# Expert stage of a two-layer diffusion block: another order of experts, one fixed in place of two, and 22 standing load places in place of 16

## Chip, cores and metric

One core of a Trainium2 chip. The metric is device time in microseconds (us) of one execution; less is better. Besides it there is one profiled execution of the kernel before, whose span runs from its first to its last instruction.

## What is computed

Two layers on 256 latent tokens of width 1024 (and 256 context tokens in the first). A layer is a mixer (linear attention beside neighbourhood attention) and a channel mixer. The change lies in the channel mixer of the second layer, a top-2-of-8 SwiGLU expert layer on the 256 latent tokens:

```python
def moe_swiglu(h, w_router, wg, wu, wd):
    def per_sample(t):
        logits = (t @ w_router).astype(jnp.float32)
        top_v, top_i = lax.top_k(logits, TOP_K)            # TOP_K = 2
        wts = jax.nn.softmax(top_v, axis=-1)
        combine = jnp.einsum('tk,tke->te', wts, jax.nn.one_hot(top_i, N_EXPERTS, ...))
        hid = jax.nn.silu(jnp.einsum('td,edf->tef', t, wg)) * jnp.einsum('td,edf->tef', t, wu)
        return jnp.einsum('tef,efd->td', hid * combine[:, :, None], wd)
```

Each of the 8 experts has three float32 matrices: gate and up 1024 x 3584, down 3584 x 1024. All 8 are read once, in units of 128 x 1024 numbers (524,288 bytes): 28 units a matrix, 84 an expert, 672 in all, 352.3 MB. After the layer follow a post-norm, a gate and the residual.

## The kernel before

**The stage.** `moe` (L1635) ends the second layer's mixer (its output projection, `out_w.run`), routes the tokens (`Router`), and then runs one `Stream` (L176) over the 672 units in the order that `Experts.jobs` (L1436) lists. A unit is loaded by SP (`wraw`, L161) into a place, and places are handed out in turn from a ring, `st.ring`; a place is free again when its unit has been read. SP issues the loads in the order of its own list, so one load that waits for its place holds back those behind it.

**Two ways to compute an expert.** *Split*: a unit is cut by ScalarE into a rounded part `wr` (L169) and by VectorE into the rest `wl` (L170), three units ahead of TensorE (`AHEAD = 3`), and six 128x512 matmuls (`mm3`, L210 to L212) multiply the two parts with the expert's tokens, which stand split in regions of `HR` and `HL` (up to 128 tokens an expert). A place is free once the unit is split. *Whole*: for an expert with at most 64 tokens, TensorE multiplies the unit as it is with 64 columns (`sides`, L1481); the trace shows four matmul records a unit. Neither ScalarE nor VectorE reads the unit, and its place is free only when TensorE has read it.

**The order.** The first `FIXED = 2` positions are experts 0 and 1. The other six are sorted by their number of tokens (`Router.rank`, L1277, which the stage steps through beside the units); `RANKS` says which rank comes at which position: few, many, few, many, few, many. "Few" positions run whole. So the order is split, split, whole, split, whole, split, whole, split. An expert from position 2 on is known to SP only by a register (`values_load` in `with_side`, L1443), read after unit 16 of the second position.

**Side work of an expert.** `gather` (L1423) picks two experts' tokens by one-hot matmuls (8 steps of four matmuls 128x256) during an earlier expert: experts 2 and 3 during the second position, 4 and 5 and then 6 and 7 during the whole ones at positions 2 and 4. The first two experts' tokens are picked together before the stage's first unit (`first`, L1389, with 256 columns). `scatter` (L1598) brings an expert's result back to its tokens; its 8 matmuls run after the second unit of the next expert, and for the last expert at once.

**Places.** 11 places are there from the mixer. At the start come 4 in pool `rm3`, 3 in `rm4`, the two accumulators, and one in `gtb`: 21. After unit 72 of the first expert `make_room` (L1724) takes the 3 in `rm4` and the 2 accumulators out: 16 from there on.

Of the kernel before, what the change touches and what calls it, by code (L numbers as in the profile page):

```python
# [25 lines left out]
FIXED = 2  # L26
RANKS = 3, 0, 4, 1, 5, 2
HALF = 64

# [58 lines left out]
ROOM_UNIT, GATHER_UNIT = 72, 32  # L88
IDS_UNIT, WHOLE_GATHER = 16, 12
RING = 4  # L90
# [3 lines left out]
def kernel(ctx: ExitStack, tc: tile.TileContext, A: dict, out: bass.AP):  # L94
# [188 lines left out]
    HR = pers.tile([P, KD, NT], F32R, name="HR")  # L283
    HL = pers.tile([P, KD, NT], F32R, name="HL")
# [847 lines left out]
    class Router:  # L1132
# [144 lines left out]
        def rank(self, pool):  # L1277
# [6 lines left out]
            def scratch():  # L1284
                return pool.tile([P, 256], F32, tag="hg", bufs=2, name="hg")

            at = scratch()[:, 0:n * n].rearrange("p (a b) -> p a b", a=n)
# [9 lines left out]
            t = scratch()[:, 0:7 * n * n].rearrange("p (q a b) -> p q a b", q=7, a=n)  # L1297
            nc.vector.tensor_tensor(out=t, in0=self.Q[:, :, FIXED:NE].unsqueeze(2).to_broadcast([P, 7, n, n]),
                                    in1=at.unsqueeze(1).to_broadcast([P, 7, n, n]), op=ALU.mult)
            nc.vector.tensor_reduce(out=self.T[:, :, FIXED:NE], in_=t, axis=AX.X, op=ALU.add)  # L1300
            yield
# [3 lines left out]
            nc.vector.tensor_scalar(out=b, in0=rank, scalar1=2.5, scalar2=-float(P - HALF), op0=ALU.is_gt, op1=ALU.mult)  # L1305
# [15 lines left out]
    class Experts:  # L1321
# [9 lines left out]
        def small(self, e):  # L1331
            return not self.rest and e >= FIXED and e % 2 == 0
# [8 lines left out]
        def region(self, e):  # L1341
            at = ((e // 2 + 1) % 2) * 256 + (e % 2) * P
            return slice(at, at + P)

        def one_hot(self, p, tts=(0, 1)):
            R, mg = self.R, self.R.mg
            for tt in tts:
                G = mg.tile([P, 2, P], F32R, tag=f"G{tt}", bufs=2, name=f"G{tt}")
                for i in range(2):
                    e = 2 * p + i  # L1350
# [4 lines left out]
                    eng, pin = (nc.gpsimd if tt else nc.vector, keep_order) if p else (nc.vector, lambda ins: ins)  # L1355
                    pin(eng.tensor_scalar(out=o, in0=io, scalar1=pos, scalar2=sel, op0=ALU.is_equal, op1=ALU.mult))
                self.G[tt] = G

        def pick(self, pg, d, tt, part, start, stop):
            nc.tensor.matmul(pg, self.R.x[tt][part][:, d * P:(d + 1) * P], self.G[tt].rearrange("p e s -> p (e s)"),  # L1360
                             start=start, stop=stop, skip_group_check=True)

        def picked(self, pg, p, d):
            at, n = self.region(2 * p).start, 256
            sc, sh = self.sc[:, d, 0:1], self.sh[:, d, 0:1]
            if self.small(2 * p):
                if d == 0:
                    self.xw[2 * p] = self.ml.tile([P, KD, HALF], F32, tag="xw", bufs=2, name="xw")
                nc.scalar.activation(self.xw[2 * p][:, d, :], pg[:, 0:HALF], AF.Identity, scale=sc, bias=sh)
                at, n, pg = at + P, P, pg[:, P:256]  # L1370
            o = (slice(None), d, slice(at, at + n))
            nc.scalar.activation(HR[o], pg, AF.Identity, scale=sc, bias=sh)
            h = self.ml.tile([P, 256], F32, tag="hg", bufs=2, name="hg")[:, 0:n]
            nc.vector.tensor_scalar(out=h, in0=pg, scalar1=sc, scalar2=sh, op0=ALU.mult, op1=ALU.add)
            nc.vector.tensor_tensor(out=HL[o], in0=h, in1=HR[o].bitcast(F32), op=ALU.subtract)

        def places(self, p):
            pt = ps()
            for i in range(2):
                for tt in range(2):  # L1380
                    o = (2 * i + tt) * P
                    nc.tensor.transpose(pt[:, o:o + P], self.G[tt][:, i, :].bitcast(F32), ident)
            gt = self.ml.tile([P, 2, 256], F32R, tag="GT", bufs=2, name="GT")
            nc.scalar.activation(gt.rearrange("p a t -> p (a t)"), pt, AF.Copy)
            self.GT[2 * p], self.GT[2 * p + 1] = gt[:, 0, :], gt[:, 1, :]
# [12 lines left out]
        def first_picked(self, places):  # L1398

            at = self.region(0).start  # L1400
            hs = [t.rearrange("p (d t) -> p d t", d=4)[:, 2 * j:2 * j + 2, :] for t in places for j in range(2)]
# [10 lines left out]
            def split(q):  # L1412
                o = (slice(None), slice(2 * q, 2 * q + 2), slice(at, at + 256))
                nc.scalar.activation(HR[o], hs[q], AF.Copy)
                nc.vector.tensor_tensor(out=HL[o], in0=hs[q], in1=HR[o].bitcast(F32), op=ALU.subtract)
# [7 lines left out]
        def gather(self, p):  # L1423
            self.one_hot(p)
            yield
            for d in range(KD):
                pg = ps()[:, 0:256]
# [3 lines left out]
                self.picked(pg, p, d)  # L1431
                yield
            self.places(p)
            yield
# [9 lines left out]
        def with_side(self, fn, e, i):  # L1444

            def g(wr, wl):
# [4 lines left out]
                if not self.rest and e == 0 and i == ROOM_UNIT:  # L1451
                    self.make_room()
                    self.places(0)
                    self.ranking = chain(self.R.weights(), self.R.rank(self.ml))
                next(self.ranking, None)
                if not self.rest and e == 1 and i == IDS_UNIT:
                    self.ids = [nc.values_load(self.R.ids[0:1, p:p + 1], engines=[mybir.EngineType.SP], min_val=0, max_val=NE - 1)
                                for p in range(NE - FIXED)]
# [3 lines left out]
                p, at = e // 2 + 1, WHOLE_GATHER if self.small(e) else GATHER_UNIT  # L1462
                if 2 * p < NE and (self.small(e) or e % 2 == 1 and (self.rest or e < FIXED)):
                    if i == at:
                        self.filler = self.gather(p)
                    if i >= at and i % 4 == 0:
                        next(self.filler, None)
# [9 lines left out]
        def expert(self, e):  # L1477
            slot, small = self.region(e), self.small(e)
            st = {}

# [30 lines left out]
            def gu(fbs, which, u, n):  # L1511
                def fn(wr, wl):
# [3 lines left out]
                    for b, fb in enumerate(fbs):  # L1516
                        for k2 in range(2 // len(fbs)):
                            kk = u * 2 // len(fbs) + k2
                            s = slice((b + k2) * 512, (b + k2 + 1) * 512)
                            if not small:  # L1520
                                mm3(st[fb, which], HR[:, kk, slot], HL[:, kk, slot], wr[:, s], wl[:, s], kk == 0, kk == KD - 1)
# [8 lines left out]
            def turn_whole(fbs):  # L1530
# [6 lines left out]
                for c in range(2 * n):  # L1537
                    st[fbs[0] * 4 + c, "x"] = t[:, c % n * P + c // n * HALF:c % n * P + (c // n + 1) * HALF]

# [58 lines left out]
        def scatter(self, e, ys):  # L1598
            small = self.small(e)
            yr = self.ml.tile([P, D], F32R, tag="yr", name="yr")  # L1600
            yl = self.ml.tile([P, D], F32R, tag="yl", name="yl")
            for half, y in enumerate(ys):
                c = slice(half * 512, (half + 1) * 512)
                nc.scalar.activation(yr[:, c], y, AF.Copy)
# [418 lines left out]
```

## Time and profile before

| | us |
|---|---|
| median of 3 runs (1928.47 to 1930.82) | 1930.63 |
| the profiled execution | 1930.77 |
| its span, first to last instruction | 1928.9 |
| expert stage: first unit's first matmul | 1003.2 |
| last expert's last unit ends on TensorE | 1914.2 |

The page gives busy time by engine and the span in 40 slices of 48.2 us. A busy TensorE there is not one at its peak, since ends of matmuls are modelled. In the expert stage the row to read beside it is GB/s, and for a stretch of one's choice the windows view (busy time by engine, granted TensorE clock, share of the DMA engines, GB/s).

### The profile page before, as it was taken

To read this page: it belongs to the slowest core of one execution; us is meant where nothing else is said; L and a number is where in the kernel's file an instruction comes from. 1 tells how busy PE (TensorE), PEld (TensorE's weight loads), DVE (VectorE), ACT (ScalarE), POOL (GpSimd) and SP (SyncE) were. 2 spreads that over 40 slices of the span, in tenths; PEclk is the share of its full clock that TensorE was granted. 3 is DMA by queue.
4 is the path that set the end of the run, shared out by engine and by line. 5 is a ranking of instruction groups with operands and counts; after the bars stand their busy time and mean duration, and the time that the engine had idled before them with its cause. 6 is when DMAs were issued, how large, how long until landed. Compare 5 with 4: busy or idle time off the path is not lost. (4 is left out here: it accounts for less than half of the span.)

```text
span 1928.9 us, 25373 instructions
## 1 busy us (share of the span) xinstructions
PE 1836.1 (95%) x8929; PEld 1296.1 (67%) x8929; DVE 1129.3 (59%) x1617; ACT 927.2 (48%) x1326; POOL 110.9 (6%) x111
## 2 busy tenths in 40 slices
PE   6999899999999998998989999998999989998997
PEld 3677557867888887786478878832786348832685
DVE  4456886432223335468789989820995149910897
ACT  4433366422222336443568778710774137710775
POOL 2001300100000002002100010100000000000000
PEclk9999999999999999999999999999999999999999
DMA  8521646175332332323889889999999999999993
GB/s 288 160 82 42 200 147 224 64 231 177 96 98 89 120 112 89 115 78 114 283 308 382 314 309 365 346 386 404 409 404 386 407 405 409 404 387 404 409 403 144
DMA packets 202182, 491.55 MB, mean 255 GB/s; under 512 B 28992, under 2 KB 70720, under 8 KB 202048
## 3 DMA queue, kind: packets, MB, share of 16 engines
q1 hardware_dynamic: 200768, 485.67, 69.2%
q0 software_dynamic: 1280, 4.20, 0.8%
q8 instruction: 72, 1.18, 0.2%
q14 instruction: 62, 0.51, 0.1%
HBM read 488.75 MB, written 4.19 MB: 256 GB/s over the span
## 5 line engine op out<-in xcount | busy, mean ns | idle before, releaser
L170 DVE TENSOR_TENSOR wl<-raw,wr 128x1024 fp32r<-128x1024 f32 x514 | 623.1, 1242 | 268.1 <-ACT wr L169 259.1
L169 ACT ACTIVATE wr<-raw 128x1024 fp32r<-128x1024 f32 x514 | 536.1, 1059 | 340.4 <-PE ps L211 135.3
L211 PE MATMUL ps<-wl,HR 128*128 128x512 f32 x736 | 291.4, 396 | 13.3 <-DVE wl L170 13.2
L210 PE MATMUL ps<-wr,HR 128*128 128x512 f32 x736 | 298.6, 406 | 3.9 <-ACT wr L169 3.9
L212 PE MATMUL ps<-wr,HL 128*128 128x512 f32 x736 | 291.8, 397 | 0.0
L210 PE MATMUL ps<-HR,wr 128*128 128x512 f32 (+1 forms) x592 | 222.2, 376 | 12.8 <-ACT HR L1863 6.0
L211 PE MATMUL ps<-HL,wr 128*128 128x512 f32 (+1 forms) x592 | 219.8, 371 | 3.4 <-POOL HL L424 1.8
L212 PE MATMUL ps<-HR,wl 128*128 128x512 f32 (+1 forms) x592 | 218.5, 369 | 0.0
L211 PEld LDWEIGHTS ps<-wl,HR 128*128 128x128 f32 x736 | 139.7, 190 | 50.2 <-DVE wl L170 19.2
L210 PEld LDWEIGHTS ps<-wr,HR 128*128 128x128 f32 x736 | 139.6, 190 | 39.8 <-ACT wr L169 6.5
L212 PEld LDWEIGHTS ps<-wr,HL 128*128 128x128 f32 x736 | 139.7, 190 | 32.7 <-issue 0.8
L1484 PE MATMUL ps<-raw,xw 128*64 128x512 f32 (+1 forms) x716 | 149.8, 548 | 9.3 <-DMA raw<-in_moe_w_gate 5.2
L210 PEld LDWEIGHTS ps<-HR,wr 128*128 128x128 f32 x592 | 111.6, 189 | 50.8 <-issue 16.0
L211 PEld LDWEIGHTS ps<-HL,wr 128*128 128x128 f32 x592 | 112.3, 190 | 24.7 <-DVE HL L1868 3.4
L212 PEld LDWEIGHTS ps<-HR,wl 128*128 128x128 f32 x592 | 112.5, 190 | 19.9
L1499 DVE TENSOR_TENSOR hid<-hid,ps 128x512 f32<-128x512 f32 (+1 forms) x47 | 31.3, 666 | 155.0 <-PE ps L1484 155.0
L211 PE MATMUL ps<-wl,tr 128*128 128x512 f32 x280 | 110.6, 395 | 1.6 <-DVE wl L170 1.5
L1484 PEld LDWEIGHTS ps<-raw,xw 128*64 128x64 f32 x716 | 46.6, 136 | 96.4 <-issue 58.3
L210 PE MATMUL ps<-wr,tr 128*128 128x512 f32 x280 | 110.7, 395 | 0.0
L212 PE MATMUL ps<-wr,tl 128*128 128x512 f32 x280 | 109.6, 391 | 0.0
L1484 PE MATMUL ps<-raw,tw 128*64 128x512 f32 x320 | 83.7, 612 | 9.2 <-DMA raw<-in_moe_w_down 7.5
L211 PEld LDWEIGHTS ps<-wl,tr 128*128 128x128 f32 x280 | 52.6, 188 | 15.6 <-DVE wl L170 4.7
(343 smaller groups left out, 2241.4 us busy)
## 6 DMA issues: line engine op xcount, KB each, us to landing
raw<-in_moe_w_up SPq DMA_DIRECT2D x212, 512.0 KB
raw<-in_moe_w_down SPq DMA_DIRECT2D x207, 512.0 KB
raw<-in_moe_w_gate SPq DMA_DIRECT2D x206, 512.0 KB
raw<-in_w_ada SPq DMA_DIRECT2D x80, 512.0 KB
raw<-in_w_in SPq DMA_DIRECT2D x48, 512.0 KB
raw<-in_ffn_w_gate SPq DMA_DIRECT2D x22, 512.0 KB
raw<-in_ffn_w_up SPq DMA_DIRECT2D x22, 512.0 KB
raw<-in_ffn_w_down SPq DMA_DIRECT2D x22, 512.0 KB
```

What stands on the lines that cost most here:

```text
L169: nc.scalar.activation(wr, raw, AF.Copy)
L170: nc.vector.tensor_tensor(out=wl, in0=raw, in1=wr.bitcast(F32), op=ALU.subtract)
L210: nc.tensor.matmul(o, lr, rr, start=start, stop=False)
L211: nc.tensor.matmul(o, lr, rl, start=False, stop=False)
L212: nc.tensor.matmul(o, ll, rr, start=False, stop=stop)
L1484: nc.tensor.matmul(o[a * HALF:(a + 1) * HALF, 0:n], x, raw[:, a * n:(a + 1) * n], start=start, stop=stop)
L1499: nc.vector.tensor_tensor(out=hid, in0=hid, in1=st.pop((fb, 1))[:, 0:w], op=ALU.mult)
```

## The change

- **One fixed expert and another order.** `FIXED` is 1, seven experts are ranked, and positions 1, 4 and 7 run whole: split, whole, split, split, whole, split, split, whole. The number of split (5) and whole (3) experts is the same.
- **Places.** `rm4` is gone, `rm3` has 6. Four places lie in the second half of `HR` and `HL` (`Halves`: the split input of the layers before is now two tiles each; the experts' regions lie in the first). At the start 11 + 6 + 2 + 1 + 4 = 24 places, 22 after unit 72.
- **Routing earlier.** Ranking begins at unit 3 of the first expert (was 72); SP reads the expert numbers after unit 76 of the first expert.
- **Side work.** Experts 1 and 2 are picked during position 0, 3 and 4 during position 1, and 5, 6 and 7 (384 columns) during position 4; before the stage's first unit only expert 0 is picked (128 columns). `scatter` keeps its split result in the buffers of `turn` (`tr`, `tl`).

```diff
-FIXED = 2
-RANKS = 3, 0, 4, 1, 5, 2
+FIXED = 1
+WHOLE = 1, 4, 7
+RANKS = 4, 0, 1, 5, 2, 3, 6
+GATHERS = {0: (1, 2), 1: (3, 4), 4: (5, 6, 7)}
+REGION = {0: 0, 2: 1, 3: 0, 5: 1, 6: 0}
...
-ROOM_UNIT, GATHER_UNIT = 72, 32
-IDS_UNIT, WHOLE_GATHER = 16, 12
-RING = 4
+RANK_UNIT, GATHER_UNIT, ROOM_UNIT, IDS_UNIT = 3, 24, 72, 76
+WHOLE_GATHER = 12
+RING = 6
...
+    class Halves:
...
+        def slots(self, r):
+            return self.tiles[0].rearrange("p k t -> p (k t)")[:, r * D:(r + 1) * D].rearrange("p (k s) -> p k s", k=KD)
+        def weights(self):
+            t = pers.tile([P, 2 * D], F32, tag=self.tags[1], name=self.tags[1] + "w")
+            return [t[:, i * D:(i + 1) * D] for i in range(2)]
+    HR, HL = Halves("HR"), Halves("HL")
...
         def small(self, e):
-            return not self.rest and e >= FIXED and e % 2 == 0
+            return not self.rest and e in WHOLE
...
         def acc(self, d):
-            return self.acc8[d // 4 * 2 + d % 2][:, (d // 2 % 2) * 256:(d // 2 % 2 + 1) * 256]
+            return self.acc8[d // 4 * 2 + d % 2][:, (d // 2 % 2) * 256:(d // 2 % 2) * 256 + P]
...
-                if not self.rest and e == 0 and i == ROOM_UNIT:
-                    self.make_room()
-                    self.places(0)
-                    self.ranking = chain(self.R.weights(), self.R.rank(self.ml))
-                next(self.ranking, None)
-                if not self.rest and e == 1 and i == IDS_UNIT:
+                if not self.rest and e == 0:
+                    if i == RANK_UNIT:
+                        self.places(0, 0)
+                        self.ranking = chain(self.R.weights(), self.R.rank(self.ml))
+                    next(self.ranking, None)
+                    if i == ROOM_UNIT:
+                        self.make_room()
+                    if i == IDS_UNIT:
...
-                    some = [(rm4.__enter__(), 3)] * 3 + [(t, 0) for t in acc]
-                    st.ring = [(rm3, RING)] * RING + some + [(gtb(), 0)] + st.ring
-                    st.load(first + RING + 6)
+                    early = [(t, 0) for t in acc]
+                    st.ring = [(rm3, RING)] * RING + early + [(t, 0) for t in [gtb()] + HR.weights() + HL.weights()] + st.ring
+                    st.load(first + RING + 7)
```

**TensorE at the end of the first expert.** (`wr`, `wl` are a split unit, `raw` and `gtb` whole ones, `yr`/`yl` the scatter, `xw` the 64 tokens, `tl` the turned hidden values.) Before, within the second expert:

```order
L210 MATMUL ps<-wr,HR 128x512
L211 MATMUL ps<-wl,HR 128x512
L212 MATMUL ps<-wr,HL 128x512
L1615 MATMUL ps<-yr,GT 128x512
L1616 MATMUL ps<-yl,GT 128x512
L1615 MATMUL ps<-yr,GT 128x512
L1616 MATMUL ps<-yl,GT 128x512
L1615 MATMUL ps<-yr,GT 128x512
L1616 MATMUL ps<-yl,GT 128x512
L1615 MATMUL ps<-yr,GT 128x512
L1616 MATMUL ps<-yl,GT 128x512
L210 MATMUL ps<-wr,HR 128x512
```

With the change, from the last matmul of the first expert on:

```order
L217 MATMUL ps<-wr,tl 128x512
L1517 MATMUL ps<-raw,xw 64x512 x4
L1650 MATMUL ps<-yr,GT 128x512
L1651 MATMUL ps<-yl,GT 128x512
L1650 MATMUL ps<-yr,GT 128x512
L1651 MATMUL ps<-yl,GT 128x512
L1650 MATMUL ps<-yr,GT 128x512
L1651 MATMUL ps<-yl,GT 128x512
L1650 MATMUL ps<-yr,GT 128x512
L1651 MATMUL ps<-yl,GT 128x512
L1517 MATMUL ps<-raw,xw 64x512 x6
L1517 MATMUL ps<-gtb,xw 64x512 x2
```

The same scatter stands after two units of the next expert, and that expert is now a whole one.

**SP's loads at the start of the stage.** (`x_65` and `x_66` are the accumulators, `HR1w` and `HL1w` the new places.) Before:

```order
L163 DMA raw<-in_moe_w_gate 128x1024 x8
L163 DMA raw<-in_moe_w_up 128x1024 x3
L163 DMA raw<-in_moe_w_gate 128x1024 x2
L163 DMA gtb<-in_moe_w_gate 128x1024
L163 DMA raw<-in_moe_w_gate 128x1024
L163 DMA x_65<-in_moe_w_gate 128x1024
L163 DMA x_66<-in_moe_w_gate 128x1024
L163 DMA raw<-in_moe_w_up 128x1024 x5
```

With the change:

```order
L168 DMA raw<-in_moe_w_gate 128x1024 x8
L168 DMA raw<-in_moe_w_up 128x1024 x3
L168 DMA HR1w<-in_moe_w_gate 128x1024 x2
L168 DMA gtb<-in_moe_w_gate 128x1024
L168 DMA HL1w<-in_moe_w_gate 128x1024
L168 DMA x_65<-in_moe_w_gate 128x1024
L168 DMA x_66<-in_moe_w_gate 128x1024
L168 DMA HL1w<-in_moe_w_gate 128x1024
L168 DMA raw<-in_moe_w_up 128x1024 x8
```

The twelfth load now goes into the split input's room, and the five up units of the first group stand behind seven others (behind five before).

**VectorE where the routing begins.** Before, late in the first expert:

```order
L170 TENSOR_TENSOR wl<-raw,wr 128x1024 x7
L1499 TENSOR_TENSOR hid<-hid,ps 128x512
L170 TENSOR_TENSOR wl<-raw,wr 128x1024
L1257 TENSOR_TENSOR oh_9184<-Q,eq_8060 128x8
L1259 TENSOR_TENSOR w_9186<-m_8056 128x1
L170 TENSOR_TENSOR wl<-raw,wr 128x1024
```

With the change, after four units of the first expert:

```order
L175 TENSOR_TENSOR wl<-raw,wr 128x1024 x4
L1284 TENSOR_TENSOR oh_8296<-Q,eq_8062 128x8
L1286 TENSOR_TENSOR w_8298<-m_8058 128x1
L175 TENSOR_TENSOR wl<-raw,wr 128x1024
L1290 TENSOR_SCALAR w_8311<-w_8298 128x1
```

The weights and the ranking of the routing moved from the end of the first expert to its beginning, between the same splits.

## Rows read from the trace of the kernel before

**Rows 1.** The page: busy time by engine; GB/s in 40 slices of 48.2 us; what was read from HBM.

```profile
PE 1836.1 (95%) x8929; PEld 1296.1 (67%) x8929; DVE 1129.3 (59%) x1617; ACT 927.2 (48%) x1326; POOL 110.9 (6%) x111
...
GB/s 288 160 82 42 200 147 224 64 231 177 96 98 89 120 112 89 115 78 114 283 308 382 314 309 365 346 386 404 409 404 386 407 405 409 404 387 404 409 403 144
...
HBM read 488.75 MB, written 4.19 MB: 256 GB/s over the span
```

**Rows 2.** Windows, one for each of the eight experts, cut where TensorE starts the expert's first matmul, and the rest of the span. Columns: stretch, its length, busy time (instructions) of PE, PEld, DVE, ACT, POOL, granted clock, DMA share, GB/s.

```profile
1003.18:1127.70 124.52, 122.47 (x540) 97.27 (x539) 111.80 (x126) 99.79 (x109) 2.25 (x2) 1.00 0.92 338
1127.70:1254.47 126.77, 126.30 (x578) 102.39 (x576) 115.59 (x126) 98.69 (x116) 9.91 (x5) 1.00 0.95 349
1254.47:1350.98 96.51, 89.99 (x427) 30.63 (x426) 12.73 (x29) 12.64 (x28) 0.00 (x0) 1.00 1.01 395
1350.98:1473.71 122.73, 121.49 (x541) 97.99 (x541) 111.13 (x103) 94.28 (x99) 0.00 (x0) 1.00 1.03 407
1473.71:1570.97 97.26, 90.22 (x428) 30.60 (x427) 12.73 (x29) 12.64 (x28) 0.00 (x0) 1.00 1.01 395
1570.97:1693.96 122.99, 122.23 (x540) 98.86 (x540) 111.23 (x103) 94.29 (x99) 0.00 (x0) 0.99 1.03 407
1693.96:1791.55 97.59, 87.12 (x391) 25.02 (x390) 6.60 (x11) 6.03 (x11) 0.00 (x0) 1.00 1.01 396
1791.55:1914.20 122.65, 121.62 (x540) 97.90 (x540) 111.05 (x103) 95.45 (x100) 0.00 (x0) 1.00 0.87 343
1914.20:1928.90 14.70, 2.69 (x9) 1.34 (x8) 8.88 (x17) 3.81 (x10) 3.24 (x1) 0.75 0.21 76
```

**Rows 3.** What SP's loads waited for: us in total, times, longest. The first row is of the first expert (1003 to 1128 us), the others of the third (1254 to 1351 us).

```profile
SPq L163 <- DVE wl L170: 74.0, 68, 8.1
...
SPq L163 <- DMA raw<-in_moe_w_down: 20.0, 27, 1.6
SPq L163 <- PE ps L1484: 13.5, 26, 3.6
```

**Rows 4.** Windows again, the same columns: the first 8 us of a whole expert that begins with its places full; 200 and 600 us in which transfers run on; the end of the transfers.

```profile
1254.00:1262.00 8.00, 8.00 (x37) 3.34 (x37) 4.61 (x8) 1.09 (x2) 0.00 (x0) 1.00 0.80 278
...
1290.00:1490.00 200.00, 192.24 (x876) 121.22 (x876) 119.68 (x122) 102.67 (x116) 0.00 (x0) 1.00 1.02 401
1490.00:1690.00 200.00, 192.20 (x878) 120.33 (x875) 118.47 (x123) 105.14 (x123) 0.00 (x0) 0.99 1.03 407
...
1290.00:1890.00 600.00, 572.95 (x2592) 348.20 (x2591) 337.51 (x340) 292.51 (x332) 0.00 (x0) 1.00 1.02 403
...
1895.00:1899.00 4.00, 4.00 (x19) 3.25 (x18) 3.86 (x5) 3.05 (x4) 0.00 (x0) 1.00 0.14 50
1899.00:1905.00 6.00, 6.00 (x30) 4.93 (x29) 5.63 (x5) 4.32 (x5) 0.00 (x0) 1.00 0.00 0
```

**Rows 5.** Timeline of PE in the fifth expert (whole): start, us, instruction. The scatter of the expert before, and ten units (40 records) after it.

```profile
1475.58 0.50 PE L1615 MATMUL ps<-yr,GT 128*128 128x512 f32 x1
...
1477.32 0.40 PE L1616 MATMUL ps<-yl,GT 128*128 128x512 f32 x1
1477.64 8.80 PE L1484 MATMUL ps<-raw,xw 128*64 128x512 f32 x40
```

**Rows 6.** The same timeline 12 us later: four picks of a gather step, then a unit, then the turning of hidden values.

```profile
1490.67 0.38 PE L1360 MATMUL ps<-G,xr 128*128 128x256 f32 x1
...
1491.34 1.08 PE L1484 MATMUL ps<-raw,xw 128*64 128x512 f32 x4
1492.35 0.66 PE L1534 MATMUL ps<-cst_base,hid 128*128 128x128 f32 x4
1492.93 2.80 PE L1484 MATMUL ps<-raw,xw 128*64 128x512 f32 x12
```

**Rows 7.** PE just ahead of the stage: the first and the last four of the 16 picks of the second token tile, the first matmul of the first expert, and the window in which the picks ran.

```profile
999.72 1.10 PE L1360 MATMUL psh<-G,xr 128*128 128x256 f32 x4 [1.06 <-DVE G L1356]
...
1002.33 1.04 PE L1360 MATMUL psh<-G,xl 128*128 128x256 f32 x4
1003.18 0.46 PE L210 MATMUL ps<-wr,HR 128*128 128x512 f32 x1
...
1000.00:1003.00 3.00, 3.00 (x16) 3.00 (x15) 1.89 (x4) 1.50 (x3) 0.00 (x0) 0.50 0.96 345
```

**Rows 8.** Timeline of ACT while the routing runs in the first expert.

```profile
1109.09 1.28 ACT L1260 ACT_TABLE_LOAD   x1
...
1115.09 0.20 ACT L1260 ACTIVATE w<-w 128x1 f32<-128x1 f32 x1 [2.61 <-DVE w L1259]
```

**Rows 9.** The end: timeline of ACT and DVE after the last unit.

```profile
1913.64 1.28 ACT L1604 ACTIVATE yr<-ps 128x512 fp32r<-128x512 f32 x2 [3.36 <-PE ps L212]
...
1914.27 1.37 DVE L1605 TENSOR_TENSOR yl<-ps,yr 128x512 fp32r<-128x512 f32 x2 [2.17 <-ACT yr L1604]
1915.55 2.75 DVE L1620 SCALAR_TENSOR_TENSOR x<-ps,T,x 128x512 f32<-128x512 f32 x4
```

**Rows 10.** Windows: 1 us just after the fifth expert (whole), and 20 us inside the seventh (whole).

```profile
1574.00:1575.00 1.00, 1.00 (x4) 0.71 (x4) 1.00 (x2) 0.91 (x1) 0.00 (x0) 0.50 1.04 418
1740.00:1760.00 20.00, 17.39 (x68) 3.65 (x68) 0.69 (x1) 1.19 (x2) 0.00 (x0) 1.00 1.02 408
```

**Rows 11.** Timeline of PE: the first matmul of a split expert after a whole one.

```profile
1570.96 0.51 PE L210 MATMUL ps<-wr,HR 128*128 128x512 f32 x1 [1.29 <-ACT wr L169]
```

More of the change, by code (lines that the diff above doesn't have):

```diff
@@ L282, with __init__, __getitem__ @@
     nc.vector.tensor_copy(selbc, B_("sel").unsqueeze(2).to_broadcast([P, 2, P]))
-    HR = pers.tile([P, KD, NT], F32R, name="HR")
-    HL = pers.tile([P, KD, NT], F32R, name="HL")
+    class Halves:
+        def __init__(self, name):
+            self.tags = [f"{name}{i}" for i in range(2)]
+            self.tiles = [pers.tile([P, KD // 2, NT], F32R, tag=t, name=t) for t in self.tags]
+        def __getitem__(self, at):
+            p, k, t = at
+            lo, hi = (k, k + 1) if isinstance(k, int) else (k.start, k.stop)
+            i = lo // (KD // 2)
+            lo, hi = lo - i * (KD // 2), hi - i * (KD // 2)
+            return self.tiles[i][p, lo if isinstance(k, int) else slice(lo, hi), t]
+        def slots(self, r):
[4 more added lines that the diff above has]
+    HR, HL = Halves("HR"), Halves("HL")
     bcol = pers.tile([P, 2, 48], F32, name="bcol")
@@ L1296, in rank @@
             self.T = mo.tile([P, 7, NE], F32, name="T")
[L1297 to L1301, printed above, removed]
+            for q in (slice(0, 3), slice(3, 6), slice(6, 7)):
+                m = q.stop - q.start
+                t = scratch()[:, 0:m * n * n].rearrange("p (q a b) -> p q a b", q=m, a=n)
+                nc.vector.tensor_tensor(out=t, in0=self.Q[:, q, FIXED:NE].unsqueeze(2).to_broadcast([P, m, n, n]),
+                                        in1=at.unsqueeze(1).to_broadcast([P, m, n, n]), op=ALU.mult)
+                nc.vector.tensor_reduce(out=self.T[:, q, FIXED:NE], in_=t, axis=AX.X, op=ALU.add)
+                yield
             self.ids = mo.tile([P, n], I32, name="ids")
@@ L1365, in picked @@
             sc, sh = self.sc[:, d, 0:1], self.sh[:, d, 0:1]
[L1366 to L1385, printed above, removed]
+            for i, e in enumerate(es):
+                if self.small(e):
+                    if d == 0:
+                        self.xw[e] = self.ml.tile([P, KD, HALF], F32, tag="xw", bufs=2, name="xw")
+                    nc.scalar.activation(self.xw[e][:, d, :], pg[:, i * P:i * P + HALF], AF.Identity, scale=sc, bias=sh)
+                else:
+                    nc.scalar.activation(self.slots(e)[0][:, d, :], pg[:, i * P:(i + 1) * P], AF.Identity, scale=sc, bias=sh)
@@ new lines, in picked, with places @@
+            for i, e in enumerate(es):
+                if not self.small(e):
+                    hr, hl = (x[:, d, :] for x in self.slots(e))
+                    h = self.ml.tile([P, 256], F32, tag="hg", bufs=2, name="hg")[:, 0:P]
+                    nc.vector.tensor_scalar(out=h, in0=pg[:, i * P:(i + 1) * P], scalar1=sc, scalar2=sh, op0=ALU.mult, op1=ALU.add)
+                    nc.vector.tensor_tensor(out=hl, in0=h, in1=hr.bitcast(F32), op=ALU.subtract)
+        def places(self, i, e):
+            pt = ps()[:, 0:256]
+            for tt in range(2):
+                nc.tensor.transpose(pt[:, tt * P:(tt + 1) * P], self.G[tt][:, i, :].bitcast(F32), ident)
+            self.GT[e] = self.ml.tile([P, 256], F32R, tag="GT", bufs=4, name="GT")
+            nc.scalar.activation(self.GT[e], pt, AF.Copy)
@@ L1398, in first_picked @@
         def first_picked(self, places):
-            at = self.region(0).start
-            hs = [t.rearrange("p (d t) -> p d t", d=4)[:, 2 * j:2 * j + 2, :] for t in places for j in range(2)]
+            hr, hl = self.slots(0)
+            hs = [t.rearrange("p (d t) -> p d t", d=4)[:, 2 * j:2 * j + 2, 0:P] for t in places for j in range(2)]
             def mod(q):
@@ L1461, in g @@
                     self.late = None
[L1462 to L1467, printed above, removed]
+                es = ((e + 1,) if e + 1 < NE else ()) if self.rest else GATHERS.get(e, ())
+                at = WHOLE_GATHER if self.small(e) else GATHER_UNIT
+                if es and i == at:
+                    self.filler = self.gather(es)
+                if es and i >= at and i % 4 == 0:
+                    next(self.filler, None)
             return g
@@ L1477, in expert @@
         def expert(self, e):
-            slot, small = self.region(e), self.small(e)
+            small = self.small(e)
             st = {}
+            if not small:
+                hr, hl = self.slots(e)
             def sides(o, x, raw, n, start, stop):
@@ L1599, in scatter @@
             small = self.small(e)
[L1600 to L1604, printed above, removed]
-                nc.vector.tensor_tensor(out=yl[:, c], in0=y, in1=yr[:, c].bitcast(F32), op=ALU.subtract)
+            yr, yl = [], []
+            for y in ys:
+                yr.append(self.mw.tile([P, 512], F32R, tag="tr", bufs=2, name="yr"))
+                yl.append(self.mw.tile([P, 512], F32R, tag="tl", bufs=2, name="yl"))
+                nc.scalar.activation(yr[-1], y, AF.Copy)
+                nc.vector.tensor_tensor(out=yl[-1], in0=y, in1=yr[-1].bitcast(F32), op=ALU.subtract)
             def late():
```

72 lines of the change are left out of this document (36 added, 36 removed).

## Prediction

> **What bounds the kernel now.** I read the page first, then windows cut at the experts, then SP's waits, then timelines. Busy TensorE says 95% of the span, which hides the point; the GB/s line shows it: from about the 27th slice on it stands at 386 to 409, below that it does not [rows 1]. So the expert stage has two halves. Cut by expert [rows 2], the rates are 338 and 349 GB/s during the first two experts (split, split) and 395 to 407 from the third to the seventh. In the first expert SP's loads wait for a place, that is for VectorE's `wl` (74.0 us); in the third they mostly wait for earlier loads to land, and only 13.5 us for TensorE [rows 3]. From the third expert on the stage runs at the pace of the transfers: 403 GB/s over 600 us [rows 4], which is 0.5243 MB / 0.403 = 1.301 us a unit.
>
> Against that stands what TensorE needs. A split expert takes about 122.7 us (1.46 a unit), slower than its transfers (109.3). A whole expert lasts 96.5 to 97.6 us [rows 2], but its units run at 8.80/10 = 0.88 us when they are there [rows 5]: 84 units are 73.9 us, the scatter 2.1 [rows 5], 8 gather steps of 0.67 are 5.4, and turnings of 0.58 add some 2.5 [rows 6]. So it needs 84 us with a gather and 78.5 without; the other 12.5 to 19 us it waits for weights. A whole expert uses up 84 units while some 65 arrive; it needs about 20 in stock, and 16 places cannot hold them. And two split experts in a row at the start keep the DMA engines waiting for places: (403-338)/403 x 124.5 = 20.1 us and (403-349)/403 x 126.8 = 17.0 us of lost transfer time.
>
> A third loss is at the end. The transfers are over by 1899 [rows 4], yet the span ends 30 us later: the last expert is a split one, TensorE is some ten units behind, and after its last unit (1914.2) come 14.7 us of scatter, norm and store [rows 2].
>
> **The change, part by part.** The amount of weights and the five split and three whole experts stay. What changes is when transfers stop, and how much is left after the last one.
>
> *Before the stage.* Of 32 picks with 256 columns the last 16 stand on the path: 999.72 to 1003.18, at the half clock [rows 7]. With 128 columns they need between half of that and all of it (no row shows this form so narrow). I take 1 us off, bounds 2 off and 0. The twelfth load now waits until the projection has read the second half of `HR`; that delays loads which the first expert needs only some 15 units later, so 0, covered by the eleven units already there.
>
> *First expert.* 124.5 us today [rows 2]. The routing was inside it and still is: a table load of 1.28 us and an exp that waits 2.61 us [rows 8] move from unit 72 to unit 3, before the first Silu, so one table load may go; I take 0, bounds -3 and +4. New is a gather of two experts, 8 x 0.67 us [rows 6]; I take 5, bounds 3.5 and 10 (should VectorE, which also splits here, become late). The second expert then starts at 1003.2 - 1 + 124.5 + 5 = **1131.7** (1127.7 before). SP's reading of the expert numbers stands between loads that wait for places anyway: 0; without that cover it would delay loads by a few us once.
>
> *From there on.* At 1131.7 the 22 places are full but for two still on their way: 84 + 20 = 104 units have landed (an estimate, from a restart of some 2.5 us and 1.3 us a unit). The second expert is now a whole one, so places come free at 0.88 us a unit, and the transfers run on instead of waiting for splits. The restart costs what it costs before the third expert today: 278 in place of 407 GB/s for 8 us [rows 4], 2.5 us. The remaining 568 units are 297.8 MB; at 403 GB/s, 738.9 us; the bounds of that rate are 401 and 407 [rows 4], 742.6 and 731.7. I add 2 us for places that fill up towards the end of a pair of split experts (0 to 5). Last landing: 1131.7 + 2.5 + 738.9 + 2 = 1875.1.
>
> The Trainium skill, "DMA: Bandwidth & Descriptors", section Specifications, speaks against this step: it puts the HBM limit of one core at about 358 GB/s. By that, an estimate, the rest would take 832 us and the run some 1988 us. This trace holds 403 GB/s for 600 us, so the measurement decides.
>
> *Does TensorE keep up?* 1131.7 + 84, 1.5 of wait at the first split [rows 11], then 122.7 + 121.4 for two split experts (the second as the second of today, 126.8 less its gather of 5.4), 86 (three experts' gather), 244.1 again, 78.5: 1869.9. That is 5 us before the last landing; both sides run nearly level, and where they take turns (each whole expert begins with some 20 units in stock and ends with none) some wait is left. For this I add 3 us: last landing 1878.
>
> *The end.* The last expert is whole, so no backlog: its last unit ends about 1.2 us after it has landed. The rest is today's 14.7 us less one of the two halves of VectorE's `yl`, which lies ahead of the four updates [rows 9]: 14.2, at best 13.5. Span: 1878 + 1.2 + 14.2 = 1893.4. The profiled execution took 1.9 us more than its span and 0.14 more than the median, so the span plus 1.7 is compared with 1930.63: **1895 us**, 36 less. All low bounds together give 1879, all high ones 1911.
>
> **The rivals.**
>
> *Only the end gains.* Transfers stop as often as before and the last landing stays at 1899; then only the backlog goes: 1899 + 1.2 + 14.2 + 1.7 = 1916. For it: the first expert still runs against full places, and places are read late by whole experts. Against it: the second expert's 17 us are lost to splits that no longer stand there. 5%.
>
> *A longer first expert.* It now holds the whole routing and a gather, and VectorE is already busy 111.8 of 124.5 us [rows 2]. 10 to 15 us more than I allow would go straight to the end, since all that follows hangs on it: 1907. 7%.
>
> *A fuller start.* If 24 places and an earlier start keep the transfers going through the first expert, up to 18 of its 20.1 us come back too: 1877. Against it: a split expert takes its units slower than they come, so places fill up whatever their number. 5%.
>
> *Slower: the clock.* Whole experts that wait for weights leave TensorE idle in small pieces. Just ahead of the stage, and for some us after the fifth expert, the granted clock is 0.50, that is 1.2 in place of 2.4 GHz, each time after TensorE had waited [rows 7, 10, 11]. At that level a whole unit takes 1.76 us, more than its transfer: (1.76 - 1.30) x 84 = 38.6 us an expert. From 36/0.46 = 78 units at the low level on, a little under one whole expert, the gain is gone; one full expert gives 1934, three 2011. Against it: in the seventh expert, with TensorE busy 17.4 of 20 us, the clock stays at 1.00 [rows 10], and the change makes such waits fewer. The Trainium skill, "TensorE: Matmul & The Clock Gate", section on HAM oscillation, names this course for thin matmuls that wait on DMA; this trace shows it outside the whole experts only. 6%, of which 4 for a full expert and more.
>
> That the places are not added, or the order not changed, is excluded by the lists of instructions. A second pass for experts with too many tokens can't start either: today 3 of 6 have at most 64 tokens, so the three fewest of 7 have too.
>
> **How the numbers follow.** Forecast 77%, the four rivals 5, 7, 5 and 6%. The forecast's own bounds (1879 to 1911) are not all met at once; the range 1884 to 1910 takes in the longer first expert and leaves out most of the fuller start, of "only the end" and of the slower case, about 2 in 10 with the edges of the forecast. A measurement of this kernel can tell about 0.2% from no change, 3.9 us. Every case but the clock is more than that below 1930.6: faster 0.94, same 0.02 (clock low for most of one whole expert), slower 0.04.
>
> **What would show it.** Windows by expert: the first 128 to 131 us; whole experts of 84 to 89 us in place of 96.5 to 97.6, with the DMA share near 1 from the second expert on, and at least 400 GB/s over the 600 us that follow 1150; transfers end near 1878, and the span 15 to 16 us later in place of 30. SP's waits from the second expert on are for landings, not for `wl`. It is wrong if the second expert starts after 1140, if the rate is under 400 in the pairs of split experts (places too few), if whole experts still last 95 us, or if the granted clock falls inside them.

## Result and profile after

The changed kernel takes 1905.36 us (median of 4 runs, 1903.81 to 1909.04) against 1929.89 for the kernel before in the same job: a ratio of 0.9876 with a 95% interval of 0.9859 to 0.9893, a gain of 24.5 us where 36 were forecast. The profiled run took 1903.81 us, its span is 1901.5.

Windows of the changed kernel, cut like [rows 2] at each expert's first matmul; the columns are the same. The last cut lies 0.3 us after the end of the last unit (1886.17), here and in the windows of the runs below that end in a whole expert:

```profile
1002.02:1132.03 130.01, 128.00 (x573) 101.83 (x574) 115.63 (x150) 100.04 (x123) 4.66 (x4) 0.99 0.95 348
1132.03:1219.64 87.61, 85.76 (x427) 32.23 (x426) 12.74 (x29) 12.81 (x28) 2.35 (x3) 1.00 1.00 395
1219.64:1342.71 123.07, 122.06 (x540) 98.10 (x541) 113.97 (x106) 97.15 (x102) 0.00 (x0) 1.00 1.03 412
1342.71:1464.24 121.53, 121.53 (x541) 98.65 (x539) 109.48 (x102) 92.52 (x98) 0.00 (x0) 1.00 1.00 388
1464.24:1553.69 89.45, 87.80 (x430) 33.31 (x429) 17.91 (x46) 15.99 (x38) 0.00 (x0) 1.00 1.00 393
1553.69:1676.70 123.01, 121.98 (x540) 98.14 (x541) 113.94 (x106) 97.11 (x102) 0.00 (x0) 1.00 1.03 411
1676.70:1798.24 121.54, 121.54 (x542) 98.67 (x540) 109.47 (x102) 92.52 (x98) 0.00 (x0) 1.00 1.00 384
1798.24:1886.50 88.26, 82.14 (x391) 27.03 (x390) 6.60 (x10) 6.47 (x11) 0.00 (x0) 1.00 0.94 373
1886.50:1901.50 15.00, 1.69 (x8) 0.85 (x8) 8.26 (x16) 3.55 (x9) 3.24 (x1) 0.68 0.20 74
```

Whole experts last 87.6 to 89.5 us instead of 96.5 to 97.6, and the span ends 15 us after the last expert's stretch, with no split expert behind the last transfers. But the rate is not level. In the first expert of each pair of split ones it is 411 to 412 GB/s, in the second 388 and 384, and in each whole one 373 to 395. The page's GB/s line (40 slices of 47.5 us) shows the two dips at the ends of the pairs, 345 in slice 31 and 345 in slice 38:

```profile
GB/s 292 162 83 42 203 139 238 39 238 198 90 96 93 120 111 56 145 89 117 215 303 360 344 327 411 411 412 409 414 387 345 409 408 414 410 412 378 345 412 262
```

What SP's loads waited for (us in total, times, longest): the first row from the first expert of the first pair (1219.6 to 1342.7 us), the second from the second expert of that pair (to 1464.2), the third from the second expert of the second pair (1676.7 to 1798.2).

```profile
SPq L168 <- DVE wl L175: 5.7, 19, 0.4
...
SPq L168 <- DVE wl L175: 53.1, 67, 1.8
...
SPq L168 <- DVE wl L175: 61.5, 78, 1.8
```

A wait for `wl` is a wait for a place. It is nearly absent in the first expert of a pair and is the largest wait in the second: the 22 places are full again. When the whole expert then begins, the transfers have to start anew. Windows of the first 8 us of the three whole experts, and of the transfers' end:

```profile
1132.00:1140.00 8.00, 8.00 (x37) 3.40 (x38) 4.62 (x8) 0.63 (x2) 0.00 (x0) 1.00 0.74 245
1464.20:1472.20 8.00, 8.00 (x37) 3.38 (x38) 4.87 (x9) 0.64 (x2) 0.00 (x0) 1.00 0.69 233
1798.20:1806.20 8.00, 8.00 (x37) 3.39 (x38) 4.11 (x6) 0.64 (x2) 0.00 (x0) 1.00 0.68 241
...
1880.00:1885.00 5.00, 3.72 (x16) 0.62 (x12) 0.00 (x0) 0.00 (x0) 0.00 (x0) 1.00 0.38 148
1885.00:1890.00 5.00, 2.77 (x12) 1.05 (x12) 2.51 (x4) 0.97 (x2) 0.00 (x0) 1.00 0.01 3
```

The last weights land at 1885.0, 7 us after the forecast 1878, and in the last 88 us TensorE is busy for 82.1 only: it waits for them.

### The profile page after: what moved, and what is told of

Read it like the earlier page. It is cut to its first block, busy times and chain, and to the rows that moved or that the text cites. A ratio compares the mean times of both kernels' runs of the same rounds, so it can differ in the third digit from the quotient of the medians.

```text
span 1901.5 us, 25591 instructions
## 1 busy us (share of the span) xinstructions
PE 1822.9 (96%) x8929; PEld 1302.0 (68%) x8929; DVE 1133.0 (60%) x1636; ACT 927.6 (49%) x1336; POOL 106.8 (6%) x112
## 5 line engine op out<-in xcount | busy, mean ns | idle before, releaser
L175 DVE TENSOR_TENSOR wl<-raw,wr 128x1024 fp32r<-128x1024 f32 x446 | 545.3, 1247 | 223.8 <-ACT wr L174 217.8
L174 ACT ACTIVATE wr<-raw 128x1024 fp32r<-128x1024 f32 x446 | 466.4, 1059 | 297.3 <-PE ps L216 135.3
L216 PE MATMUL ps<-wl,HR 128*128 128x512 f32 x736 | 292.0, 397 | 13.7 <-DVE wl L175 13.4
L1517 PE MATMUL ps<-raw,xw 128*64 128x512 f32 (+1 forms) x596 | 117.2, 536 | 1.6 <-DMA raw<-in_moe_w_gate 0.9
L1532 DVE TENSOR_TENSOR hid<-hid,ps 128x512 f32<-128x512 f32 (+1 forms) x47 | 31.3, 665 | 131.2 <-PE ps L1517 131.2
L1517 PEld LDWEIGHTS ps<-raw,xw 128*64 128x64 f32 x596 | 40.7, 137 | 66.0 <-issue 53.9
L1517 PE MATMUL ps<-raw,tw 128*64 128x512 f32 x272 | 65.6, 602 | 4.1 <-DMA raw<-in_moe_w_down 2.5
L217 PEld LDWEIGHTS ps<-wr,tl 128*128 128x128 f32 x280 | 52.5, 188 | 12.8
```

Of the source, the lines that this page charges most:

```text
L174: nc.scalar.activation(wr, raw, AF.Copy)
L175: nc.vector.tensor_tensor(out=wl, in0=raw, in1=wr.bitcast(F32), op=ALU.subtract)
L216: nc.tensor.matmul(o, lr, rl, start=False, stop=False)
L217: nc.tensor.matmul(o, ll, rr, start=False, stop=stop)
L1517: nc.tensor.matmul(o[a * HALF:(a + 1) * HALF, 0:n], x, raw[:, a * n:(a + 1) * n], start=start, stop=stop)
L1532: nc.vector.tensor_tensor(out=hid, in0=hid, in1=st.pop((fb, 1))[:, 0:w], op=ALU.mult)
```

## Experiments

The theory after this reading (A): TensorE's work is as forecast; every pair of split experts ends with all places full, so a whole expert begins with as many units in stock as there are places, plus the cost of a restart, and for the rest it waits. The rivals are that the order alone brought the gain, and that the longer whole experts are TensorE's own work. Spans are best compared from the stage's first matmul on, since its beginning differs between runs (1001.3 to 1006.8): 899.5 us for the changed kernel (1901.5 - 1002.0).

**The order with the old 16 places.**

```diff
-RING = 6
+RING = 4
...
-                    st.ring = [(rm3, RING)] * RING + early + [(t, 0) for t in [gtb()] + HR.weights() + HL.weights()] + st.ring
-                    st.load(first + RING + 7)
+                    st.ring = [(rm3, RING)] * RING + early + [(t, 0) for t in [gtb()]] + st.ring
+                    st.load(first + RING + 3)
```

> The new order with the old number of places: the four places in the split input's room and two of the six in rm3 are left out, so 16 stand after unit 72 of the first expert, as before. Theory A (places): wherever a whole expert begins with all places full, each place fewer is one unit less in stock and costs one transfer, 1.3 us; that happens at three whole experts, so 3 x 6 x 1.3 = 23 us on top of 1905: 1928 (1918 to 1932), the order alone gains almost nothing; the rates of the second split experts of the pairs fall from 388 and 384 to 360 to 375 GB/s, whole experts last 92 to 97 us. Theory B (order): the gain comes from the order of the experts, places hardly matter: 1905 (1901 to 1910).

Measured: 1928.69 us, ratio to before 0.9988 (0.9978 to 0.9998). Windows, two second split experts of a pair and the three whole ones:

```profile
1350.00:1473.36 123.36, 123.36 (x550) 100.13 (x548) 110.96 (x104) 93.98 (x100) 0.00 (x0) 1.00 0.97 364
...
1692.00:1814.37 122.37, 122.37 (x546) 99.33 (x544) 110.12 (x103) 93.33 (x99) 0.00 (x0) 1.00 0.98 362
...
1133.16:1228.78 95.62, 89.95 (x427) 30.72 (x427) 12.74 (x29) 12.81 (x29) 2.35 (x3) 1.00 1.01 397
1473.36:1569.91 96.55, 91.40 (x430) 32.05 (x429) 17.92 (x46) 15.98 (x38) 0.00 (x0) 1.00 1.00 394
1814.37:1910.10 95.73, 86.62 (x391) 25.20 (x390) 6.60 (x10) 6.46 (x11) 0.00 (x0) 1.00 0.96 379
```

The whole experts are 8.0, 7.1 and 7.5 us longer than with 22 places, 1.26 us a place: A holds, and the order alone is worth 0.12%. The order takes the stops for places out of the second expert and puts others at the end of each pair.

**The places with the old order.**

```diff
-FIXED = 1
-WHOLE = 1, 4, 7
+FIXED = 2
+WHOLE = 2, 4, 6
```

`RANKS`, `GATHERS` and `REGION` follow this order.

> The old order (split, split, whole, split, whole, split, whole, split; two fixed experts) with all the rest of the change: 22 places, early routing, the new places of the picks. Theory A: places fill up only once, at the end of the two split experts at the start, so six more places give 6 x 1.3 = 7.8 us once; the first expert takes 3 to 5 us more for routing and a gather: 1925 (1921 to 1929). Rival: every whole expert has 7.8 us less to wait: 1909. Rival: the end is set by TensorE's backlog in the last split expert, and nothing comes of it: 1930 to 1934.

Measured: 1927.17 us, 0.9983 (0.9972 to 0.9994). The first whole expert and the next one:

```profile
1256.80:1345.29 88.49, 86.20 (x428) 32.05 (x427) 12.74 (x29) 12.83 (x29) 1.57 (x2) 1.00 1.00 392
...
1468.48:1565.25 96.77, 89.88 (x428) 30.74 (x427) 12.74 (x29) 12.83 (x29) 0.00 (x0) 1.00 1.03 406
```

Only the first is much shorter than in [rows 2], by 8.0 us; the next is 0.5 us shorter and the last whole one 1.9, since one split expert alone does not fill the places: SP waited 3.3 us for `wl` in the split expert between these two, against 83.4 us in the split expert ahead of the first. The first two experts together take 255.0 us instead of 251.3. So each half of the change is worth 0.1 to 0.2%, and both together 1.24%: the order makes three stops at full places, and only more places make a stock of them.

**A split expert at the end.** `RANKS` and `REGION` follow.

```diff
-WHOLE = 1, 4, 7
+WHOLE = 1, 4, 6
```

> As the changed kernel, but the last two experts are exchanged: split, whole, split, split, whole, split, whole, split, so that a split expert ends the stage. Theory A: no places fill up behind the fifth expert any more, so the transfers end some 6 us earlier (about 1878), but TensorE is then a dozen units behind: the last split expert begins when the whole one's last unit has landed (about 1771) and takes 122.7 us; 1894 + 15 + 2 = 1911 (1907 to 1916). Rival: only the transfers decide, the kind of the last expert doesn't: 1899.

Measured: 1913.95 us, 0.9911 (0.9897 to 0.9924). The last weights land at 1882.0, some 5 us earlier counted from the stage's start (1004.0 here; 6 forecast), and TensorE ends 15 us after them:

```profile
1774.40:1897.20 122.80, 121.78 (x539) 97.89 (x540) 111.25 (x103) 95.19 (x100) 0.00 (x0) 1.00 0.84 337
```

The whole expert at the end is worth 8.6 us, although with it the transfers end 5 us later, counted from the stage's start.

**Scatter later in a whole expert.**

```diff
-                if i == 1 and self.late is not None:
+                if i == (9 if self.small(e) else 1) and self.late is not None:
```

> As the changed kernel, but in a whole expert the scatter of the expert before it runs after unit 9 instead of unit 1. Theory A: the 3.4 us that a restart of the transfers costs hold 2.1 us in which TensorE scatters and frees no place; with the scatter later each of the three restarts is up to 2 us shorter: 1899 to 1902, and the first 8 us of the fifth and eighth expert at 280 to 340 GB/s instead of 234 and 243. Rival: the restart is the time from a place's release to the landing of its load, whatever TensorE does between: 1905.

Measured: 1902.11 us, 0.9862 (0.9841 to 0.9883), 894.3 us from the stage's start, 5.2 less than the changed kernel. The first 8 us of the three whole experts, and each of them in full:

```profile
1132.40:1140.40 8.00, 8.00 (x39) 2.78 (x40) 1.38 (x2) 1.25 (x3) 0.00 (x0) 1.00 0.76 266
1464.30:1472.30 8.00, 8.00 (x39) 2.74 (x40) 1.38 (x2) 1.19 (x2) 0.00 (x0) 1.00 0.88 327
1795.30:1803.30 8.00, 8.00 (x39) 2.78 (x40) 1.38 (x2) 1.20 (x3) 0.00 (x0) 1.00 0.89 329
...
1132.45:1219.26 86.81, 85.32 (x428) 32.37 (x427) 12.75 (x29) 12.79 (x29) 2.34 (x3) 1.00 1.00 398
1464.26:1551.40 87.14, 87.14 (x429) 33.54 (x429) 18.71 (x46) 16.60 (x39) 0.00 (x0) 1.00 1.01 403
1795.30:1881.40 86.10, 81.78 (x391) 27.13 (x390) 6.59 (x10) 6.48 (x12) 0.00 (x0) 1.00 0.97 384
```

The restarts of the fifth and the eighth expert run at 327 and 329 GB/s, as forecast; the one of the second expert rises from 245 to 266 only. The three experts are 0.8, 2.3 and 2.2 us shorter. So about the 2.1 us of the scatter, in which no place comes free, lay in two of the restarts. The 0.8 us of the second expert is no more than the same window differs between two runs with the early scatter (87.6 and 88.7 us), so for it the gain is not shown. The four times lie far apart (1898.64 to 1908.52), so the medians alone (1905.36, 1902.11) would not separate the two kernels. The rates do: all nine restarts in the three profiled runs with the late scatter (this one and two below) have 266 to 331 GB/s in their first 8 us, all nine in three with the early one (the changed kernel and two below) 224 to 258.

**Four more places from the fifth expert on.**

```diff
...
+                if not self.rest and e == 4 and i == 64:
+                    self.more_room()
...
+                    def more_room():
+                        st.ring = [(mg.tile([P, D], F32, tag=f"x{a}{tt}", name=f"x{a}{tt}w"), 0) for a in "rl" for tt in range(2)] + st.ring
```

> As the changed kernel, but from unit 64 of the fifth expert on the four tiles of normalised tokens (xr0, xr1, xl0, xl1), whose last gather is done by then, serve as four more places: 26 for the second pair of split experts and the last expert. Theory A: the second pair's transfers stop later, its second expert runs at 395 to 405 GB/s instead of 384, the last expert begins with four units more in stock and lasts 4 x 1.3 = 5 us less (83 us from its first matmul to its last, was 88); span 1896 to 1897, 1900 us (1898 to 1903). Rival (the transfers as a whole are the limit, a fuller stock only moves the wait): 1905, the last expert 88 us.

Measured: 1899.20 us, 0.9829 (0.9816 to 0.9842). The second expert of the second pair, and the last expert:

```profile
1677.70:1799.70 122.00, 122.00 (x544) 99.06 (x542) 109.78 (x103) 92.99 (x99) 0.00 (x0) 1.00 1.02 402
1799.70:1882.20 82.50, 79.72 (x391) 27.82 (x390) 6.59 (x10) 6.45 (x11) 0.00 (x0) 1.00 0.95 375
```

402 instead of 384 GB/s, and 5.8 us off the last expert with four places: A again, 1.4 us a place.

**Accumulators as places for longer.** In addition to the late scatter, the two accumulators stay in the ring until unit 3 of the second expert.

```diff
-                    if i == ROOM_UNIT:
-                        self.make_room()
...
+                if not self.rest and e == 1 and i == 3:
+                    self.make_room()
```

> As the variant with the late scatter, and the two accumulators stay places for five units of the second expert, up to its units 5 and 6 (24 places at its start instead of 22). Theory A: the second expert waits some 2.5 us for weights there; two units more in stock take 2 us of it, the rest of the kernel is shifted and not changed, since the places are full again at the end of each pair: span 1894 to 1895, 2 us under the late scatter alone (1896.4). Rival: the start of the last expert decides alone, 1896.4 again.

Measured: 1899.43 us, 0.9831 (0.9817 to 0.9844). The second expert shrinks from 86.8 to 85.65 us, less than the 2 expected, and the last expert lasts 87.4 instead of 86.1. From the stage's start it is 894.4 us against 894.3 with the late scatter alone, so the profile shows no gain, and the span of 1897.3 us misses the forecast of 1894 to 1895. The medians are 2.7 us apart, but the times of the late scatter alone spread over 10 us, so they do not decide it. Why the last expert took 1.3 us longer is open.

**A region with its rows apart.** `slots` returns every other 128 columns instead of one block.

```diff
-            return self.tiles[0].rearrange("p k t -> p (k t)")[:, r * D:(r + 1) * D].rearrange("p (k s) -> p k s", k=KD)
+            return self.tiles[0].rearrange("p k t -> p (k t)").rearrange("p (k a s) -> p k a s", k=KD, a=2)[:, :, r, :]
```

> As the changed kernel, but an expert's tokens stand in a region with 256 columns between the rows of 128, as before, instead of one block. Tests whether the split experts' 0.5 us each over those of the old kernel (123.2 to 123.7 against 122.7 to 123.0 where the old order runs with the new regions) come from the layout. If so, split experts of 122.7 and 121.4 us and 1902 to 1903; if not, no difference: 1905, 123.1 and 121.5.

Measured: 1907.29 us, 0.9872 (0.9857 to 0.9887); the pairs last 246.1 and 244.6 us instead of 244.6 both, and not the 244.1 that the layout as cause would give. The layout is not shown to be the cause; half a microsecond a split expert stays unexplained.

**TensorE without late weights.**

```diff
+                if self.extra and k >= 84 and k % 2:
+                    self.raw[k] = self.raw[k - 1]
+                    continue
                 src, a = self.jobs[k][0]
```

> As the changed kernel, but from the second expert on only every other unit is loaded and each loaded unit is used twice (half of the weights are left out, so its output isn't the reference's): TensorE, ScalarE and VectorE do the same work, the transfers can no longer be late. It measures the term 'does TensorE keep up' by itself. Forecast's sum: whole experts of 84, 86 and 78.5 us, pairs of 244.1, last unit ended at about 1870, span about 1885. With the pairs as measured (244.6) and 1 us at each change from whole to split: 1872, span 1887. Rival (the longer whole experts are not waits for weights but TensorE's own work, gather and scatter): 87.6, 89.4 and 88 us as in the changed kernel, span 1901.

The profiled execution, the only one, has a span of 1881.8 us, 3 less than the forecast's sum, since a pair takes 242.6 us and not 244.1. Windows from the second expert on, the two split experts of a pair in one:

```profile
1131.55:1216.36 84.81, 84.81 (x428) 32.56 (x427) 16.22 (x31) 14.59 (x30) 2.35 (x3) 1.00 0.79 254
1216.36:1458.92 242.56, 242.56 (x1082) 196.73 (x1080) 220.05 (x204) 187.64 (x197) 0.00 (x0) 1.00 0.62 187
1458.92:1546.06 87.14, 87.14 (x429) 33.55 (x429) 21.39 (x48) 17.77 (x40) 0.00 (x0) 1.00 0.77 239
1546.06:1788.61 242.55, 242.55 (x1082) 196.72 (x1080) 220.03 (x204) 187.65 (x197) 0.00 (x0) 1.00 0.62 188
1788.61:1866.20 77.59, 77.30 (x391) 28.74 (x390) 6.60 (x10) 6.42 (x12) 0.00 (x0) 1.00 0.42 136
```

TensorE's own work is 734.7 us, and it is busy without a gap until the last expert. Against the changed kernel's windows the waits for weights there are 2.8 us in the second expert, 2.3 in the fifth, 10.7 in the last, and 2.0 in each pair: 19.8 together. The rival that the whole experts are long by themselves falls.

**The parts together.** Late scatter, accumulators kept longer and four more places in one kernel.

```diff
...
-                    if i == ROOM_UNIT:
-                        self.make_room()
...
-                if i == 1 and self.late is not None:
+                if not self.rest and e == 4 and i == 64:
+                    self.more_room()
+                if i == (9 if self.small(e) else 1) and self.late is not None:
...
+                if not self.rest and e == 1 and i == 3:
+                    self.make_room()
...
```

> Late scatter, accumulators kept as places into the second expert, four more places from the fifth expert's unit 64 on. Theory A: the parts add up, since each shortens another whole expert's wait: span 1896.4 - 2 - 5 = 1889 to 1890, 1892 us (1890 to 1896). Rival: once the restart is shorter the transfers run level with TensorE and more places bring nothing: span 1894 to 1896.

Measured: 1892.26 us (1890.74 to 1896.84), 0.9793 (0.9780 to 0.9807), faster than both kernels. The profiled run was the slowest of the five and its stage began at 1006.8; from there it is 888.0 us, against 894.3 with the late scatter alone: 6.3 less where 7 were forecast, of which 5.3 lie in the last expert. The whole experts, and the second pair:

```profile
1137.00:1222.62 85.62, 84.88 (x427) 32.57 (x426) 12.74 (x29) 12.79 (x28) 2.34 (x3) 1.00 1.01 395
...
1467.18:1554.37 87.19, 87.19 (x429) 33.56 (x428) 17.91 (x46) 15.96 (x37) 0.00 (x0) 1.00 1.01 401
1554.37:1798.79 244.42, 243.37 (x1082) 196.87 (x1080) 223.45 (x207) 189.67 (x199) 0.00 (x0) 1.00 1.02 407
1798.79:1879.60 80.81, 78.50 (x391) 28.23 (x390) 6.59 (x10) 6.44 (x12) 0.00 (x0) 1.00 0.96 383
```

85.6, 87.2 and 80.8 us stand against 84.8, 87.1 and 77.6 without late weights: little is left to wait for.

## Why the prediction was right, and where it was off

**Start of the second expert: right.** 1132.0 against 1131.7, and 130.0 us for the first expert against 129.5. Inside it the terms differ. Windows cut at its units 24 and 72, before and then after:

```profile
1003.18:1038.51 35.33, 34.87 (x154) 27.66 (x153) 32.20 (x33) 30.33 (x35) 0.00 (x0) 1.00 1.00 380
1038.51:1106.45 67.94, 67.94 (x306) 55.63 (x305) 62.12 (x58) 54.24 (x57) 0.00 (x0) 1.00 0.90 332
1106.45:1127.70 21.25, 19.66 (x84) 13.98 (x82) 17.48 (x37) 15.22 (x18) 2.25 (x2) 1.00 0.84 282
```

```profile
1002.02:1042.17 40.15, 38.14 (x157) 28.26 (x158) 34.99 (x64) 30.10 (x38) 3.06 (x2) 0.97 0.96 354
1042.17:1114.70 72.53, 72.53 (x341) 59.86 (x340) 67.50 (x76) 59.42 (x75) 1.60 (x2) 1.00 0.93 340
1114.70:1132.03 17.33, 17.33 (x77) 13.71 (x76) 13.14 (x12) 10.53 (x11) 0.00 (x0) 1.00 0.98 368
```

The stretch to which the routing moved is 4.8 us longer, the one it left 3.9 shorter; the stretch with the gather is 4.6 longer (5 forecast). Routing at nothing was right as a balance. That the start agrees to 0.3 us is in part luck: the stage's first matmul lies between 1001.3 and 1006.8 in the profiled runs, and the first expert took 131.2 us in the run with its rows apart.

**TensorE's sum: right.** 738.2 us forecast from the second expert on; 734.7 without late weights. The clock stayed at 1.00 in every whole expert, so the slower rival did not come; no run here shows its price of 1.76 us a unit. No whole expert in any run here shows the course that the Trainium skill, "TensorE: Matmul & The Clock Gate", section on HAM oscillation, describes for thin matmuls that wait on DMA. That does not speak against the section: in the changed kernel's last expert, TensorE's waits for weights come in pieces of about 1 us at most, and longer ones were not tried.

**Transfers: the step that was off, with three sizes wrong, partly against each other.** The step from 1131.7 to the last landing put 738.9 us for 568 units, 2.5 for one restart, 2 for full places and 3 for interplay: 746.4. Measured are 753.0.
- *The rate.* 403 GB/s [rows 4] was a mean over whole and split experts, which already held small losses. While places come free in time it is 412: 297.8 MB take 723 us, 16 less than forecast. It does not stop at 358, the figure of the Trainium skill, "DMA: Bandwidth & Descriptors", section Specifications.
- *"2 us for places that fill up".* This is the mis-sized term. (412-388)/412 x 121.5 = 7.1 and (412-384)/412 x 121.5 = 8.3: 15.4 us, outside its bounds of 0 to 5.
- *The restart and the end.* The restart was charged once, at the second expert, and comes three times, since each pair ends with full places. The first 8 us at 245, 233 and 241 GB/s in place of 412 cost 3.2, 3.5 and 3.3 us, 10.0 together. The same sum over the whole experts in full gives 3.6 + 4.1 + 6.9 = 14.6 us up to the last landing, against 2.5 and the 3 for interplay. Of the rest, 3.2 us are the last 5 us of the transfers, at 148 GB/s: a term that the prediction left out, though the transfers of the kernel before ran out in the same way [rows 4].

723 + 15.4 + 14.6 = 753. This is an account of one trace, bytes at 412 GB/s and what each window lost against that, so it has to add up; that the second term hangs on the places is shown by the runs with 16 and 26 of them, and the late scatter shows part of the third. Against the prediction the three make -16, +13.4 and +9.1 us. That only 7 are left of them is luck.

**The end: right in kind, 1.1 us short.** Timeline of the last unit and what follows:

```profile
1885.57 0.60 PE L1517 MATMUL ps<-raw,tw 128*64 128x512 f32 x2
1886.27 0.60 ACT L1639 ACTIVATE yr<-ps 128x512 fp32r<-128x512 f32 x1 [12.13 <-PE ps L1517]
1886.90 0.69 DVE L1640 TENSOR_TENSOR yl<-ps,yr 128x512 fp32r<-128x512 f32 x1 [17.07 <-ACT yr L1639]
...
1888.18 2.73 DVE L1655 SCALAR_TENSOR_TENSOR x<-ps,T,x 128x512 f32<-128x512 f32 x4 [0.58 <-PE ps L1651]
```

One half of `yl` is gone, as forecast, but nothing is saved: before, the first half's sum was complete ahead of the last unit's end, and its `yr` began at 1913.64, under the last matmuls [rows 9]. Now one sum holds both halves, and `yr`, `yl` and a matmul stand one after the other: the updates begin 2.0 us after the last unit instead of 1.35, so the tail is 15.3 us instead of 14.2.

**The sum of it.** Last unit +7.0, tail +1.1; the median lies 3.9 us above the profiled span where 1.7 was taken. That is the 10.4 us between 1895 and 1905.4.

**Its own signs.** Most of what the prediction named came: 130.0 us for the first expert, 402 GB/s over 600 us, whole experts of 87.6 to 89.5 us (84 to 89 forecast), and a span that ends 16.5 us after the last landing (15 to 16 forecast). Two signs did not. SP waits for `wl` again in the second expert of each pair, and over the second pair the rate is under the 400 GB/s below which the prediction called itself wrong, with too few places as the reason. So the range held, but the picture of transfers that run on from the second expert to the end did not. Windows of the 600 us and of the second pair:

```profile
1150.00:1750.00 600.00, 594.45 (x2721) 413.35 (x2718) 430.64 (x441) 371.90 (x426) 2.35 (x3) 1.00 1.02 402
...
1553.69:1798.24 244.55, 243.52 (x1081) 196.81 (x1081) 223.41 (x207) 189.63 (x199) 0.00 (x0) 1.00 1.02 398
```

## What to carry to other kernels

An order of work and the room for its stock are one change: either alone gained 0.1 to 0.2% here, both 1.2%. Follow the stock through every cycle, not only the first: where it reaches its limit again, both the full places and the restart behind them have to be charged each time, at the rate of a stretch without stops. And work that frees no place, like a scatter, does not belong into the first units after a stop: here it cost some 2 us at two of three.

## What was not expected of the hardware

Transfers ran at 411 to 412 GB/s for over 120 us while TensorE, ScalarE and VectorE were busy with a split expert, with a DMA share of 1.03. No expert of the kernel before is above 407, at the same share [rows 2]. The number of places is not the reason: a split expert of the new order with 16 places (first line) runs at 410, one of the old order with 22 places (second line) at 407.

```profile
1570.00:1692.00 122.00, 120.99 (x537) 97.40 (x538) 113.20 (x105) 96.29 (x101) 0.00 (x0) 1.00 1.03 410
...
1345.29:1468.48 123.19, 122.06 (x540) 98.00 (x540) 111.53 (x103) 94.47 (x99) 0.00 (x0) 1.00 1.03 407
```

So in these runs the faster rate came with the order; what in it brings the 1% is open.
